# The sums of weight blocks on GpSimd, and output steps 3.5 units behind their load

## The chip, the core and the metric

The kernel runs on one core of a Trainium2 chip. The core has a matrix engine (TensorE, PE in the profile; its weight loads are PEld), a vector engine (VectorE, DVE), an activation engine (ScalarE, ACT), a general engine (GpSimd, POOL) and an engine that mostly issues transfers (SyncE, SP). Each takes its instructions in a fixed order and waits for the others through semaphores. Transfers between HBM and the on-chip memory (SBUF) are issued from the queues of SP, ACT or POOL; an instruction that stands behind a waiting one in such a queue waits with it. TensorE writes its sums to a small second memory (PSUM). The metric is the time of one execution on the device in microseconds (us).

## The reference

The kernel computes one step of a decoder layer for a prompt of 2048 tokens and 8 single-token samples, with a model width of 1024, in float32. Cut to what matters here:

```python
ada = silu(c) @ w_ada + b_ada                        # shift, scale, gate
hn = rmsnorm(x, g_norm) * (1 + scale) + shift
z = hn @ w_in                                        # xa, za | q, k, v, glr, zg
# group 1, RG-LRU: conv of 4 over xa, two gates, h_t = a_t * h_(t-1) + u_t
y_lru = h * silu(za)
# group 2, GLA: 4 heads, S_t = diag(alpha_t) S_(t-1) + k_t^T v_t, o_t = q_t S_t
y_gla = rmsnorm(o) * g_gla_norm * silu(zg)
mix = concatenate([y_lru, y_gla]) @ w_out
y = rmsnorm(x + gate * mix, g_final)
```

The final state of both groups is returned too, for the prompt and for the samples.

## The kernel before, in words

Every float32 product is made from three products of shortened numbers: each operand is split into a high part and a rest (`hh` and `hl` for the activations, two halves of a tile `w` for the weights), and high x high, high x rest and rest x high are added in PSUM. Lines 346 to 348 and 663 to 665 are these three for the values and for the other projections, line 1571 for the products of a later stage, line 1858 for the output product.

The prompt is worked on in two halves of 1024 tokens. In each half four heads of GLA (`gla_head`, in the order 3, 0, 1, 2) follow each other, and some tiles of 128 channels of the RG-LRU (`lru`) stand behind each head. A tile of the RG-LRU is projected (`project`, L663 to L665), convolved on VectorE (`conv`, L1286 and L1288), split (`xh`, `xl`, L1305 and L1306 or L1312 and L1313), sent through two gate products (`gates`, L1325 to L1328) and through a scan over the tokens (L1344). In the second half the samples' states are loaded too: per head two loads of four samples (`sample_state`, L1106 and L1108), each scaled on ScalarE (L1112) and VectorE (L1113) and used by TensorE (L1122). Between the halves the operands of some projections are put together (`gates_seven`, `lru_seven`). At the end comes the output product over the whole prompt (`Pair`, L1858).

Two places use the block form with seven products in place of eight for a 2 x 2 product of matrices. It needs sums and differences of the four blocks of a weight matrix, and these are what this document is about.

- `pair_weights` does it for six pairs of column blocks of `w_in`, in the first half. A pair is loaded to `tr` (L774, on GpSimd's queue). Then come three groups of operations: four differences (`sub`, L778), and twice two splits (`split`), each a copy `th` on ScalarE (L783), a difference on VectorE (L784) and two stores to `twd` on GpSimd's queue (L786). After the last group the next pair is loaded.
- `out_weights` does it for `w_out`, in 16 steps, six in the first half and ten in the second. `begin` (steps 0, 6 and 8) loads the gate `g` and a bias (L811, L812), which `add` sums (L817). `load` brings four blocks of 128 x 256 to `r` (L831). Then `step` multiplies them by the gate (two operations over 128 x 512, L852) in one group, and forms four differences (128 x 256, L852) in a second. Steps 4 to 7 and 12 to 15 have a third group with two splits (`p`; L856 on ScalarE, L857 on VectorE, stores on L859). `store` writes the results to `wd` (L866, on GpSimd's queue), and `again` loads the next step's blocks. The stores of the last step have to land before the output phase can load its first weights (`load_w`, L1722), as these take the same place in SBUF. The split of these weights (L1708 on ScalarE) is in the list ahead of some of the last splits of the RG-LRU.

When an operation enters the program is set by an order written out by hand. `after(units, fn)` puts `fn` into a list with a due time; `tick(units)` moves the clock on, by 1 after most projections and by 0.5 after a tile of values, and runs all entries that are due by then, in the order of due time and, at the same due time, of entry:

```python
def tick(units=1.0):
    clock[0] += units
    while pend and pend[0][0] <= clock[0]:
        heapq.heappop(pend)[2]()
```

A unit is about 24 matmuls, some 6 to 8 us. Two helpers tie a group to the place at which it enters. `behind(V)` keeps the VectorE operations inside it behind the last VectorE operation that is in the program so far, in VectorE's own order. `held(V)` makes each instruction inside it that GpSimd or SyncE executes or issues wait by a semaphore for that last VectorE operation.

In the first half the output steps end with the stop that `lru_last_a` sets. The step in work is carried to its end there, and `close_sp` starts the remaining ones in the second half. At the end of the second half the list is emptied until the last step has been stored.

Of the kernel before, what the change touches and what calls it, by code (L numbers as in the profile page):

```python
# [8 lines left out]
F32 = mybir.dt.float32  # L9
# [3 lines left out]
OP = mybir.AluOpType  # L13
# [36 lines left out]
def dram(ap, off, pattern):  # L50
    return bass.AP(tensor=ap.tensor, offset=ap.offset + off, ap=pattern)
# [3 lines left out]
def hybrid_kernel(ctx, tc, i, o):  # L55
    nc = tc.nc
    V, S, G, PE, SP = nc.vector, nc.scalar, nc.gpsimd, nc.tensor, nc.sync
# [625 lines left out]
    def behind(q):  # L683

        return tc.issue_after(next(x for x in reversed(list(nc.cur_bb.bb.instructions)) if x.engine == q.engine))


    @contextmanager
    def held(q):

        traced = nc.cur_bb.bb.instructions
        mark = next(x for x in reversed(list(traced)) if x.engine == q.engine)
        before = {id(x) for x in traced}
        yield
        for x in list(traced):
            if id(x) not in before and x.engine in (SP.engine, G.engine):
                tc.add_manual_dep(x, mark.name, mybir.DependencyInfo(
                    mybir.DependencyClass.Sync, mybir.DependencyReason.DATA), reason="held")
# [4 lines left out]
    def after(units, fn, gla=False):  # L703
        clock[1] += 1
        heapq.heappush(pend, (clock[0] + units, clock[1], fn, gla))
# [46 lines left out]
    def ready(what):  # L752
        nonlocal hp
        waiting.remove(what)
        if what == "pairs":
            hpx.close()
            hp = hpx.enter_context(tc.tile_pool(name="hp", bufs=1, reuse_waits="tile"))
        if not waiting:
            out_weights()

    def zpairs():

        return ([(ZG + 2 * h * P, ZG + (2 * h + 1) * P) for h in HEADS[1:]]
                + [(ZA + j * P, XA + j * P) for j in EARLY])

    def pair_weights(n=0):

        cols = zpairs()
        if n == len(cols):
            ready("pairs")  # L770
            return
        r = hp.tile([P, 2, KT, P], F32, tag="tr", name="tr")
        for a, col in enumerate(cols[n]):
            G.dma_start(r[:, a], i["w_in"][0, :, col:col + P].rearrange("(k p) n -> p k n", p=P))  # L774
        b11, b21, b12, b22 = r[:, 0, :4], r[:, 0, 4:], r[:, 1, :4], r[:, 1, 4:]

        def sub(x, y, z):
            return lambda: V.tensor_tensor(x, y, z, op=OP.subtract)  # L778

        def split(k, x):  # L780
            def f():
                t = hp.tile([P, 4, P], F32R, tag="th", name="th", bufs=2)
                S.copy(t, x)  # L783
                V.tensor_tensor(x, x, t.bitcast(F32), op=OP.subtract)  # L784
                for u, y in enumerate((t.bitcast(F32), x)):
                    G.dma_start(twd[n, k, :, u], y.rearrange("p k n -> p (k n)"))  # L786
            return f

        def one(ops):
            for f in ops[0]:  # L790
                with behind(V):
                    f()
            if ops[1:]:
                after(0.5, lambda: one(ops[1:]))
            else:
                pair_weights(n + 1)

        halves = [split(k, x) for k, x in enumerate((b11, b22, b12, b21))]
        after(4, lambda: one([[sub(b11, b12, b11), sub(b12, b22, b12), sub(b22, b22, b11), sub(b21, b21, b22)],
                                halves[:2], halves[2:]]))  # L800

    def out_weights(s0=0):


        def begin(s):
            q = s // 8
            outw["busy"] = True

            g = hp.tile([P, 2, 256], F32, tag="g", name="g")
            bt = hp.tile([P, 2, 256], F32, tag="t", name="bt")  # L810
            G.dma_start(g, dram(gated, (8 + 32 * q) * 256, [[0, P], [64 * 256, 2], [1, 256]]))  # L811
            G.dma_start(bt, dram(i["b_ada"], 2 * D + q * 256, [[0, P], [512, 2], [1, 256]]))  # L812
            r = load(s)

            def add():
                with behind(V):
                    V.tensor_tensor(g, g, bt, op=OP.add)  # L817
                after(0.5, lambda: step(s, r, g))

            after(4, add)  # L820

        def where(s):

            return s // 8, s // 4 % 2, s % 4

        def load(s):
            q, f, m = where(s)
            r = hp.tile([P, 2, 2, 256], F32, tag="r", name="r")
            for a in range(2):
                k = CTS[f] + 4 * a + m  # L830
                G.dma_start(r[:, a], i["w_out"][0, k * P:(k + 1) * P].rearrange("p (b n) -> p b n", b=2)[:, :, q * 256:q * 256 + 256])  # L831
            return r

        def one(ops, end):


            with behind(V):
                for f in ops[0]:
                    f()
            if ops[1:]:  # L840
                after(0.5, lambda: one(ops[1:], end))
            else:
                end()

        def step(s, r, g):
            t = hp.tile([P, 3, 256], F32, tag="t", name="t")
            b11, b12, b21, b22 = r[:, 0, 0], r[:, 0, 1], r[:, 1, 0], r[:, 1, 1]
            q, f, m = where(s)
            c = slice(q * 256, q * 256 + 256)

            def op(*a):
                return lambda: V.tensor_tensor(*a[:3], op=a[3])  # L852

            def split(n, x):
                p = hp.tile([P, 2, 256], F32R, tag="p", name="p", bufs=2)
                S.copy(p[:, 0], x)  # L856
                V.tensor_tensor(p[:, 1], x, p[:, 0].bitcast(F32), op=OP.subtract)  # L857
                for h in range(2):
                    G.dma_start(wd2[n, :, h, m, c], p[:, h].bitcast(F32))  # L859

            def store():

                for x, ops in ((r[:, 0], (B11, T1)), (r[:, 1], (B21, B22)), (t, (T2, T3, T4))):
                    for n, k in enumerate(ops):
                        if not (f and k in (B22, T4)):
                            G.dma_start(wd[f, k, :, m, c], x[:, n])  # L866
                if outw["stop"] or s == 15:
                    outw["busy"], outw["next"] = False, s + 1
                elif s % 8 < 7:
                    again(s + 1, g)  # L870
                elif q == 0:
                    begin(s + 1)

            one([[op(r[:, 0], r[:, 0], g, OP.mult), op(r[:, 1], r[:, 1], g, OP.mult)],
                 [op(t[:, 1], b22, b12, OP.subtract), op(b12, b12, b11, OP.subtract),
                  op(t[:, 0], b22, b12, OP.subtract), op(t[:, 2], b21, t[:, 0], OP.subtract)]]
                + ([[lambda: split(0, b22), lambda: split(1, t[:, 2])]] if f else []), store)

        def again(s, g):
            r = load(s)  # L880
            after(4, lambda: step(s, r, g))

        begin(s0)

# [855 lines left out]
    class Pair:  # L1740
# [157 lines left out]
        def end(self, t):  # L1898
            V.scalar_tensor_tensor(self.z[t], self.z[t], self.r[:, t:t + 1], gfin, op0=OP.mult, op1=OP.mult)
# [70 lines left out]
    for x in pairs[:2]:  # L1970
        x.new(A11)
        r = wp.tile([P, 1088], F32, tag="wr", name="wr")[:, :D].rearrange("p (q k t) -> p q k t", q=2, k=4)
# [215 lines left out]
    for n in range(2, 16):  # L2188
        g = n - 1
        x, prev = pairs[n], pairs[n - 1]  # L2190
# [16 lines left out]
    for q in range(8):  # L2207
        g, k = 2 + q // 2, q % 2
# [63 lines left out]
```

## Time and profile before

| what | value |
| --- | --- |
| median of the runs shown | 1492.54 us (1488.46 to 1494.33, 3 runs) |
| profiled execution, its own time | 1491.94 us |
| its span in the profile | 1490.2 us |
| mean granted clock of TensorE | 0.985 |
| TensorE busy | 1436.1 us, 96% |
| VectorE busy | 1058.3 us, 71% |
| ScalarE busy | 692.2 us, 46% |
| GpSimd busy, its transfer issues counted | 225.3 us, 15% |

The profile is of one execution. Its page gives the busy time of each engine and a line of 40 slices, each slice 37 us long, with the busy share in tenths; `PEclk` is the clock that TensorE was granted, in tenths of full speed. Other views group instructions by their line, list what an engine waited for, or give the instructions in order of time. `L852` is line 852 of the kernel. `r<-r,g` reads: the tile `r` is written from `r` and `g`. The busy time of VectorE, ScalarE and GpSimd counts where TensorE, which is busy nearly always, waits for them.

### The profile page before, as it was taken

The page shows a single profiled execution, that of the slowest core. Times are in us where ns is not written, and L with a number is a line of the kernel's source. Part 1 is how long each engine was busy: PE and PEld are TensorE (multiplying, and loading weights), DVE is VectorE, ACT ScalarE, POOL GpSimd, SP SyncE. Part 2 cuts the span into 40 slices and gives each one's busy share as a digit, 9 for nine tenths or more (in the row PEclk, how much of TensorE's full clock was granted, in tenths as well). Part 3 has the DMA queues.
Part 4 walks back from the last instruction along what each step waited for, and adds up shares of the span by engine and source line. Part 5 has one row for each costly group of instructions (what it writes and reads, how often), then busy time and mean ns, then how long its engine had stood idle before and what let it go on. Part 6 is the DMA issues. An engine that isn't in the chain of part 4 may idle for free.

```text
span 1490.2 us, 23612 instructions
## 1 busy us (share of the span) xinstructions
PE 1436.1 (96%) x8729; PEld 1256.3 (84%) x8729; DVE 1058.3 (71%) x2488; ACT 692.2 (46%) x1255; POOL 225.3 (15%) x374
## 2 busy tenths in 40 slices
PE   8999999999999999999999999999978999999998
PEld 6888989888898988788899998998977787778886
DVE  5757667666666779844559777686867797588886
ACT  4654544653445467533455454444437432244342
POOL 1200112211121112000212332332310000000000
PEclk9999999999999999999999999999998999999999
DMA  9655867765666454757855665565561757793452
GB/s 330 251 180 187 284 222 234 233 233 169 196 203 215 147 179 171 247 201 237 293 162 195 178 233 177 189 204 188 198 200 63 278 205 273 266 350 116 147 174 113
DMA packets 164040, 310.05 MB, mean 208 GB/s; under 512 B 13202, under 2 KB 91698, under 8 KB 161485
## 3 DMA queue, kind: packets, MB, share of 16 engines
q1 hardware_dynamic: 108197, 218.96, 42.9%
q0 software_dynamic: 23680, 73.59, 15.0%
q10 hardware_dynamic: 32048, 16.00, 3.6%
q8 instruction: 69, 1.13, 0.3%
q14 instruction: 46, 0.38, 0.1%
HBM read 191.13 MB, written 117.42 MB: 207 GB/s over the span
## 4 chain that ended last, share of the span: by engine, by line
PE 58%; DVE 15%; issue 11%; DMA 7%; ACT 7%; POOL 2%; POOLq 0%; SPq 0%; DVEq 0%; ACTq 0%
PE acc L1858 10%; PE tp L1858 7%; PE acc L663 7%; PE acc L665 7%; PE acc L664 7%; PE acc L1571 7%; PE acc L346 2%; PE acc L347 2%; PE acc L348 2%; DMA w<-wd 1%; DMA xt<-in_state_gla_dram 1%; PE po L1084 1%; DVE cv L1288 1%; DVE tg L1344 1%; ACT L989 1%
## 5 line engine op out<-in xcount | busy, mean ns | idle before, releaser
L663 PE MATMUL acc<-hh,w 128*128 128x512 f32 (+3 forms) x1080 | 375.9, 348 | 1.3 <-DVE mid L1015 1.1
L664 PE MATMUL acc<-hl,w 128*128 128x512 f32 (+3 forms) x1080 | 365.0, 338 | 0.2 <-DVE hl L205 0.2
L665 PE MATMUL acc<-hh,w 128*128 128x512 f32 (+3 forms) x1080 | 364.5, 337 | 0.0
L663 PEld LDWEIGHTS acc<-hh,w 128*128 128x128 f32 x1080 | 204.8, 190 | 19.2 <-DVE mid L1015 1.4
L664 PEld LDWEIGHTS acc<-hl,w 128*128 128x128 f32 x1080 | 205.2, 190 | 16.8 <-DVE hl L205 0.5
L665 PEld LDWEIGHTS acc<-hh,w 128*128 128x128 f32 x1080 | 204.7, 190 | 16.4 <-issue 0.4
L1858 PE MATMUL acc<-w,a 128*128 128x512 f32 (+1 forms) x792 | 186.8, 389 | 3.4 <-ACT a L1708 3.3
L1858 PEld LDWEIGHTS acc<-w,a 128*128 128x128 f32 x792 | 147.7, 189 | 37.8 <-ACT a L1708 3.7
L346 PE MATMUL acc<-w,hh 128*128 128x256 f32 (+1 forms) x508 | 145.4, 286 | 1.8 <-DMA w<-parts 1.8
L347 PE MATMUL acc<-w,hh 128*128 128x256 f32 (+1 forms) x508 | 144.1, 284 | 0.0
L348 PE MATMUL acc<-w,hl 128*128 128x256 f32 (+1 forms) x508 | 143.4, 283 | 0.0
L1858 PE MATMUL tp<-w,a 128*128 128x512 f32 x564 | 136.3, 391 | 0.4 <-DVE w L1711 0.4
L1858 PEld LDWEIGHTS tp<-w,a 128*128 128x128 f32 x564 | 105.2, 188 | 27.5 <-issue 5.2
L346 PEld LDWEIGHTS acc<-w,hh 128*128 128x128 f32 x508 | 96.6, 190 | 3.8 <-DMA w<-parts 2.0
L348 PEld LDWEIGHTS acc<-w,hl 128*128 128x128 f32 x508 | 96.8, 191 | 0.1
L347 PEld LDWEIGHTS acc<-w,hh 128*128 128x128 f32 x508 | 96.4, 190 | 0.2
L1136 ACT ACTIVATE zs<-acc 128x512 f32<-128x512 f32 (+3 forms) x70 | 34.3, 490 | 100.5 <-PE acc L665 96.8
L1288 DVE SCALAR_TENSOR_TENSOR cv<-xa,vecT,cv 128x512 f32<-128x512 f32 (+2 forms) x120 | 76.3, 642 | 6.3 <-ACT cv L1286 6.0
L1708 ACT CAST a<-s 128x512 fp32r<-128x512 f32 x61 | 36.5, 619 | 94.6 <-issue 31.6
L1137 DVE SCALAR_TENSOR_TENSOR zs<-zs,acc 128x512 f32<-128x512 f32 (+3 forms) x70 | 38.4, 549 | 44.4 <-ACT zs L1136 44.4
L965 ACT CAST vh<-acc 128x256 fp32r<-128x256 f32 x56 | 20.6, 371 | 95.0 <-PE acc L348 81.1
L966 DVE TENSOR_TENSOR vl<-acc,vh 128x256 fp32r<-128x256 f32 x56 | 23.4, 421 | 53.7 <-ACT vh L965 53.6
(404 smaller groups left out, 2813.5 us busy)
## 6 DMA issues: line engine op xcount, KB each, us to landing
parts<-w SPq DMA_DIRECT2D x37, 1024.0 KB
w<-parts SPq DMA_DIRECT2D x26, 1024.0 KB
wr<-in_w_in_dram SPq DMA_DIRECT2D x38, 512.0 KB
a<-mixd SPq DMA_DIRECT2D x63, 256.0 KB
w<-twd SPq DMA_DIRECT2D x24, 512.0 KB
w<-wd SPq DMA_DIRECT2D x12, 1024.0 KB
w<-parts SPq DMA_DIRECT2D x18, 512.0 KB
mixd<-zs ACTq DMA_DIRECT2D x35, 256.0 KB
```

The costliest lines, as they stand in the source:

```text
L346: PE.matmul(ps, hh[:, kt, c], hi[:, kt % 4], start=kt == 0, stop=False)
L347: PE.matmul(ps, hh[:, kt, c], lo[:, kt % 4], start=False, stop=False)
L348: PE.matmul(ps, hl[:, kt, c], hi[:, kt % 4], start=False, stop=kt == KT - 1)
L663: PE.matmul(ps[:, :n], hi[:, kt], a, start=kt == 0, stop=False)
L664: PE.matmul(ps[:, :n], hi[:, kt], b, start=False, stop=False)
L665: PE.matmul(ps[:, :n], lo[:, kt], a, start=False, stop=kt == KT - 1)
L1136: S.activation(z, ps, AF.Tanh, scale=0.5)
L1137: V.scalar_tensor_tensor(z, z, 1.0, ps, op0=OP.add, op1=OP.mult)
L1288: V.scalar_tensor_tensor(cv[:, cq], xa[:, cq.start + k:cq.stop + k], cw[k], cv[:, cq], op0=OP.mult, op1=OP.add)
L1571: PE.matmul(ps, w[:, u, k], x[v][k], start=start and (k, u, v) == (0, 0, 0), stop=(k, u) == (3, 1), skip_group_check=True)
L1708: S.copy(t[:, 0, k], (low(t) if src is None else src)[:, k])
L1858: PE.matmul(ps, t[:, u, k], w[:, v, k, c], start=(q < 3 or ps is own) and (k, u, v) == (0, 0, 0), stop=(k, u) == (3, 1), skip_group_check= ...
```

## The change

All operations of the two block-sum helpers that ran on VectorE or ScalarE run on GpSimd. The copies that ScalarE made by `copy` are made by a `tensor_scalar` that multiplies by one and adds zero. The groups are tied by `held(V)` in place of `behind(V)`, so that GpSimd waits at each group for the last VectorE operation before it. In `pair_weights` the whole group now stands under one `held(V)`, stores included, and the groups are 1 unit apart in place of 0.5. In `out_weights` a step is due 3.5 units behind its load in place of 4; the groups of a step are still 0.5 apart, and the wait of 4 units in `begin` stays.

```diff
         def sub(x, y, z):
-            return lambda: V.tensor_tensor(x, y, z, op=OP.subtract)
+            return lambda: G.tensor_tensor(x, y, z, op=OP.subtract)
 
         def split(k, x):
             def f():
                 t = hp.tile([P, 4, P], F32R, tag="th", name="th", bufs=2)
-                S.copy(t, x)
-                V.tensor_tensor(x, x, t.bitcast(F32), op=OP.subtract)
+                G.tensor_scalar(t, x, 1.0, 0.0, op0=OP.mult, op1=OP.add)
+                G.tensor_tensor(x, x, t.bitcast(F32), op=OP.subtract)
                 for u, y in enumerate((t.bitcast(F32), x)):
                     G.dma_start(twd[n, k, :, u], y.rearrange("p k n -> p (k n)"))
             return f
 
         def one(ops):
-            for f in ops[0]:
-                with behind(V):
+            with held(V):
+                for f in ops[0]:
                     f()
             if ops[1:]:
-                after(0.5, lambda: one(ops[1:]))
+                after(1, lambda: one(ops[1:]))
             else:
                 pair_weights(n + 1)
...
             def add():
-                with behind(V):
-                    V.tensor_tensor(g, g, bt, op=OP.add)
+                with held(V):
+                    G.tensor_tensor(g, g, bt, op=OP.add)
                 after(0.5, lambda: step(s, r, g))
...
-            with behind(V):
+            with held(V):
                 for f in ops[0]:
                     f()
...
             def op(*a):
-                return lambda: V.tensor_tensor(*a[:3], op=a[3])
+                return lambda: G.tensor_tensor(*a[:3], op=a[3])
 
             def split(n, x):
                 p = hp.tile([P, 2, 256], F32R, tag="p", name="p", bufs=2)
-                S.copy(p[:, 0], x)
-                V.tensor_tensor(p[:, 1], x, p[:, 0].bitcast(F32), op=OP.subtract)
+                G.tensor_scalar(p[:, 0], x, 1.0, 0.0, op0=OP.mult, op1=OP.add)
+                G.tensor_tensor(p[:, 1], x, p[:, 0].bitcast(F32), op=OP.subtract)
                 for h in range(2):
                     G.dma_start(wd2[n, :, h, m, c], p[:, h].bitcast(F32))
...
         def again(s, g):
             r = load(s)
-            after(4, lambda: step(s, r, g))
+            after(3.5, lambda: step(s, r, g))
```

## The prediction

> **What bounds the kernel now.** I read the page first (engines, then the slices), then the waits of TensorE, then the granted clock by stretches, and last the rows around each long wait.
>
> ```profile
> PE 1436.1 (96%) x8729; PEld 1256.3 (84%) x8729; DVE 1058.3 (71%) x2488; ACT 692.2 (46%) x1255; POOL 225.3 (15%) x374
> PE   8999999999999999999999999999978999999998
> PEclk9999999999999999999999999999998999999999
> ```
>
> TensorE is busy for 96% of the span, with two thinner slices near three quarters of it (1118 to 1192 us). VectorE at 71% and GpSimd at 15% bound nothing as a whole. Whatever the change does to VectorE, ScalarE and GpSimd reaches the end only through an idle stretch of TensorE. Inside the blocks' stages (143 to 1110 us) and just behind them, the long ones are these, in TensorE's timeline (start, length, work, in brackets the idle time before it and what ended it):
>
> ```profile
> 276.70 1.22 PE L1325 MATMUL acc<-xh,wg 128*128 128x512 f32 x2 [3.18 <-ACT xh L1312]
> 924.86 1.08 PE L1122 MATMUL po<-xt,qm 128*32 128x256 f32 x8 [3.08 <-DVE xt L1113]
> 1029.00 0.94 PE L1050 MATMUL tp<-xb,e 128*128 128x128 f32 x6 [2.69 <-DVE xb L1035]
> 1090.05 0.64 PE L1122 MATMUL po<-xt,qm 128*32 128x256 f32 x8 [2.91 <-DVE xt L1113]
> 1120.79 1.01 PE L1325 MATMUL acc<-xh,wg 128*128 128x384 f32 x2 [8.16 <-ACT xh L1305]
> ```
>
> Each costs more than its idle time. By stretches (us, then busy time of PE, PEld, DVE, ACT, POOL, the granted clock, DMA share, GB/s):
>
> ```profile
> 276.80:282.40 5.60, 5.60 (x13) 4.38 (x14) 4.90 (x14) 4.60 (x7) 0.89 (x1) 0.50 0.68 190
> 1030.00:1033.40 3.40, 3.40 (x13) 3.40 (x12) 1.72 (x6) 3.35 (x8) 0.73 (x1) 0.50 0.92 304
> 1091.40:1094.80 3.40, 3.40 (x13) 3.39 (x12) 2.31 (x12) 3.37 (x5) 0.00 (x0) 0.50 0.48 165
> 1120.80:1128.90 8.10, 7.47 (x22) 5.83 (x23) 6.17 (x11) 7.15 (x15) 0.00 (x0) 0.50 0.21 87
> ```
>
> The reader is to see the 0.50 behind each idle stretch: at half clock half of the stretch is lost, 2.8 us at 277, 1.7 at 1030, 1.7 at 1091, 4.0 at 1121. A wait of 2.7 us thus costs about 4.4. The Trainium skill (TensorE: Matmul & The Clock Gate, Part 1) says that activity is judged in free-running windows of about 3.4 us; the two 3.4 us rows agree, and by it an idle stretch of this size loses the clock only if it lies unluckily.
>
> **The change part by part.** Taken off: busy time of seven lines over the whole run (same columns, but of that line alone, so the time stands under DVE or ACT): L778, L784, L817, L852, L857 on VectorE, then L783, L856 on ScalarE.
>
> ```profile
> 0.00:1490.20 1490.20, 16.49 (x24) 0.99 0.62 208
> 0.00:1490.20 1490.20, 15.68 (x24) 0.99 0.62 208
> 0.00:1490.20 1490.20, 2.05 (x3) 0.99 0.62 208
> 0.00:1490.20 1490.20, 47.48 (x96) 0.99 0.62 208
> 0.00:1490.20 1490.20, 6.46 (x16) 0.99 0.62 208
> 0.00:1490.20 1490.20, 14.74 (x24) 0.99 0.62 208
> 0.00:1490.20 1490.20, 6.47 (x16) 0.99 0.62 208
> ```
>
> So 88.2 us leave VectorE and 21.2 leave ScalarE, of the 1490. By shape (from the code) that is, in two-input operations, 48 + 3 + 32 = 83 of 512 columns and 64 + 16 = 80 of 256; in copies 24 of 512 and 16 of 256.
>
> Put on GpSimd: a one-input operation of 512 columns has rows, and so has what happens when VectorE works at the same time. GpSimd, then VectorE, both in the timeline:
>
> ```profile
> 582.08 1.12 POOL L204 TENSOR_SCALAR hh<-fs 128x512 fp32r<-128x512 f32 x1 [1.23 <-ACT fs L201]
> 600.05 0.62 POOL L204 TENSOR_SCALAR hh<-fs 128x512 fp32r<-128x512 f32 x1 [1.34 <-DVE fs L203]
> ```
>
> ```profile
> 581.31 0.74 DVE L1288 SCALAR_TENSOR_TENSOR cv<-xa,vecT,cv 128x512 f32<-128x512 f32 x1
> 582.05 0.68 DVE L205 TENSOR_TENSOR hl<-fs,hh 128x512 fp32r<-128x512 f32 x1
> 582.65 1.09 DVE L1288 SCALAR_TENSOR_TENSOR cv<-xa,vecT,cv 128x512 f32<-128x512 f32 x1
> ```
>
> Alone the operation takes 0.62 us. Started beside a two-input VectorE operation it takes 1.12, about until that one ends (582.05 + 0.68) plus its own 0.62, and the next VectorE operation then takes 1.09 in place of 0.74. The two engines take turns. No row shows a two-input operation on GpSimd: it lies between 0.62 (as one input) and 1.24 us (two inputs read in turn), 0.31 to 0.62 for 256 columns; I take the upper ends, since the row has one operand to fetch and the new form two. That is 83 x 1.24 + 80 x 0.62 + 24 x 0.62 + 16 x 0.31 = 102.9 + 49.6 + 14.9 + 5.0 = 172 us on GpSimd, and by the lower ends 96. The Trainium skill (GPSIMD Engine Reference, elementwise side by side) has 4497 ns for 2048 columns of a two-input add; as an estimate 1.12 us for 512, and 157 us in all. What that does to VectorE is read from the stages:
>
> ```profile
> 143.00:340.00 197.00, 190.02 (x1270) 170.81 (x1269) 136.52 (x296) 103.84 (x178) 37.85 (x63) 0.98 0.70 232
> 366.00:556.00 190.00, 190.00 (x1053) 165.88 (x1052) 132.25 (x284) 92.21 (x151) 35.92 (x63) 1.00 0.58 189
> 990.00:1110.00 120.00, 113.88 (x833) 109.04 (x833) 89.86 (x309) 53.65 (x121) 35.90 (x62) 0.97 0.59 193
> ```
>
> In the first, VectorE works 136.5 of 197 us, 32 of them on the blocks; what stays is 104, or 0.53. If GpSimd's 172 us meet a VectorE that wants the port for half of the time, VectorE loses some 90 us and has been given 88: a wash in load. The bounds are a gain of 88 (they never meet) and a loss of 84 (they always do). In the first stage GpSimd's share is 48 x 1.24 + 24 x 0.62 = 74 us; at worst VectorE is at (104 + 74) / 197 = 0.90 and GpSimd at (38 + 74) / 197 = 0.57, so neither becomes the bound. The cover is TensorE's other products: in the second stage it is busy for 190.0 of 190 us beside all this. What is left is single places.
>
> The pace: the order list counts units and looks at its entries at each tick, mostly a whole unit. A wait of 1 in place of 0.5 between the groups of a pair therefore ends at the same tick, but the entry then stands behind gates due at that tick, not ahead. 3.5 in place of 4 changes nothing where a step's last group ended on a whole unit and no half tick follows; by the ticks it moves steps 2 to 5 and 11 to 15 ahead by half a unit or one, up to some 8 us. Their r loads and stores on GpSimd's queue move with them. The first six steps still fall before the stop, so that work is not redistributed. All this costs nothing while no TensorE operand comes from it; where it does:
>
> (a) 276 us. VectorE loses one block operation (0.7) and ScalarE two copies (1.2) from the chain to `xh`: -1.8. But the groups now sit behind the gates' last operations, beside the convolution that ends the wait: a copy, a two-input operation and another copy, 0.62 + 1.24 + 0.62 = 2.5. Net +0.7; bounds -4.6 (the wait falls to 1.4 and the 2.8 of half clock go) and +2.5.
>
> (b) 924 and 1090 us. Both wait for the second state load, which stands in GpSimd's queue behind a step's stores and next loads:
>
> ```profile
> 915.54 1.44 POOL L831 DMA_DIRECT2D r<-in_w_out_dram  x2 [2.50 <-DMA wd<-r]
> 916.97 0.78 POOL L1108 DMA_DIRECT2D xt<-in_state_gla_dram  x1
> 1078.01 1.44 POOL L831 DMA_DIRECT2D r<-in_w_out_dram  x2
> 1080.62 0.76 POOL L1108 DMA_DIRECT2D xt<-in_state_gla_dram  x1
> ```
>
> At 916 the step keeps its tick (step 9). Its four subtractions take 4 x 0.62 = 2.5 us on GpSimd, ahead of the stores, where stores now slip in between; the state load and TensorE come later by 1.5 (0 to 3.5). At 1078 step 14 is one tick earlier, so its loads have passed: -2 (0 to -4.6, the wait under 1.5 and the 1.7 of half clock gone).
>
> (c) 1029 us. Two products with the gate stand in VectorE right ahead of `xb`:
>
> ```profile
> 1027.19 1.28 DVE L852 TENSOR_TENSOR r<-r,g 128x512 f32<-128x512 f32 x2
> 1028.39 0.55 DVE L1035 SCALAR_TENSOR_TENSOR xb<-acc,xb 128x384 f32<-128x384 f32 x1
> ```
>
> Without them the wait is 1.5, and the 1.7 of half clock may go: -2.9. But they now run a tick earlier on GpSimd, 2 x 1.24, possibly ahead of the state load of that place, whose arrival starts the same chain: then +1.3. I take -1.
>
> (d) The last step, 1121 us. The chain of waits, with GpSimd's last issue and SyncE's wait:
>
> ```profile
> 1108.48 1.07 POOL L859 DMA_DIRECT2D wd<-p  x2 [0.88 <-ACT p L856]
> SPq L1722 <- DMA wd<-p: 5.0, 1, 5.0
> 1113.38 5.19 DMA w<-wd
> 1118.67 1.14 ACT w L1708 x2
> ```
>
> ```profile
> 1097.49 0.69 DVE L852 TENSOR_TENSOR r<-r,g 128x512 f32<-128x512 f32 x1
> 1098.10 1.23 DVE L1341 SCALAR_TENSOR_TENSOR tg<-xl,tg 128x1032 f32<-128x1032 f32 x1
> 1101.33 2.35 DVE L1344 TENSOR_TENSOR_SCAN tg<-xl,hc,tx 128x1024 f32<-128x1024 f32 x1
> ```
>
> The first weights of the last phase are loaded (5.2 us) when the last step's stores have landed, as they take its place; ScalarE splits them ahead of `xh`, and TensorE has stood for 8.16 us. Now the two products start a tick earlier. The other eight operations (4 x 0.62 + 2 x 0.31 + 2 x 0.62 = 4.3 us) alternate with VectorE's long ones, and seven stores of 0.54 follow or slip between: 8.1 us from 1097.5 (where VectorE has the step's work now) if nothing blocks, and 13.5 if each operation waits out one of VectorE's (8 x 0.7, an estimate between 0.69 and 2.35), so the last issue ends between 1105.6 and 1111.0 (now 1109.6). I take the later end, as VectorE has no pause there: +1.4 on the wait and +1 of half clock, +2.4 (-4 to +5).
>
> (e) New short waits where GpSimd holds the port for 1.24 us and VectorE held itself for 0.68: +1 (0 to +8).
>
> Sum: 0.7 + 1.5 - 2 - 1 + 2.4 + 1 = +2.6 on the profiled run's 1491.9 (span 1490.2 and 1.7 around it): 1494.5. The median of the runs shown is 1492.5, 0.6 above that run.
>
> **The rivals.** Faster: the port turns are hidden and the three middle waits fall under 2 us, without their half clock: -4.6, -2.9, -4.6 make -12, with (d) as forecast about -10, so 1482. For it: all three lie within 3.2 us. Against: GpSimd's work returns to the same spots.
>
> Slower through the last step: only (d). From where the stores land 4 us later, the wait is 12.2 and one or two more stretches of 3.4 us run at half clock: +4 +1.7 to 3.4, near 1500. Then it decides alone; 1497 to 1502. For it: VectorE's unbroken row there. Against: the earlier products.
>
> Slower through the port: an engine twice as slow holds it longer, and in the convolution chains of 143 to 340 and 870 to 1110 us three new waits of 2.7 us appear, each with 1.7 of half clock: 3 x 4.4 = +13, so 1505. The Trainium skill (SBUF — State Buffer, Who interferes with whom) calls the pair of ports that the two share an exclusive lock for the whole instruction; the 1.12 and 1.09 above agree. Against: from 366 to 556 us TensorE has no idle time at all, so most waits there have slack.
>
> **How the numbers follow.** A measurement of this kernel tells about 0.5%, 7.5 us, from no change. Forecast (within 0.5%) 0.47; faster 0.20; last step 0.15; port 0.15; slower in a way not listed 0.03. The likeliest one's own range is 1487 to 1500. For 8 in 10 the range reaches into both sides: 1481 to 1508. Faster 0.20, same 0.47, slower 0.33.
>
> **What would show it.** VectorE's busy time down by less than 88 us, with single two-input operations near 1.2 to 1.9 us; GpSimd's up by 150 to 220 with waits inside; two-input 512-column operations there at 1.1 to 1.3 us where alone; the idle stretch before `xh` near 1121 us 8 to 11 us long; those at 1029 and 1090 shorter. I am wrong if two-input operations on GpSimd take far from 1.2 us, if a new wait of over 2.7 us stands between 366 and 556 us, or if TensorE's matmuls themselves grow.

## The result, and the profile after

The changed kernel takes 1507.6 us (median of 4 runs, 1504.4 to 1509.4) against 1490.5 (4 runs) for the kernel before: a ratio of 1.011, 95% interval 1.008 to 1.014. It is slower by 16 to 17 us. The span of the profiled execution grew from 1490.2 to 1506.5 us.

The page of the kernel after, engines and slices:

```profile
PE 1440.1 (96%) x8729; PEld 1255.7 (83%) x8729; DVE 1061.3 (70%) x2325; ACT 673.2 (45%) x1215; POOL 439.4 (29%) x577
PE   8999998799999999999999999989996999999998
PEclk9999999899999999999999999999998999999999
```

VectorE's instructions fell from 2488 to 2325, but its busy time did not fall: 1061.3 us against 1058.3. Without the 88.2 us that the moved operations had cost there (five of the seven lines, the other two ran on ScalarE) it would be about 970, so some 91 us were added to other instructions. GpSimd grew by 214 us. TensorE has a new thin place at slices 7 and 8 (226 to 301 us), and a lesser one at slice 27 (979 to 1017).

TensorE's timeline of the kernel after, with the rows that answer to those of before and most of the longest new ones (start, length, instruction, in brackets the idle time and what ended it):

```profile
240.91 0.39 PE L1080 MATMUL po<-vh,amh 128*128 128x256 f32 x1 [2.93 <-DVE on L1089]
258.88 1.33 PE L1170 MATMUL tp<-ident,on 128*128 128x128 f32 x6 [1.68 <-DVE on L1097]
286.73 0.80 PE L1325 MATMUL acc<-xh,wg 128*128 128x512 f32 x1 [7.86 <-ACT xh L1312]
935.70 0.64 PE L1122 MATMUL po<-xt,qm 128*32 128x256 f32 x8
1002.85 0.88 PE L1170 MATMUL tp<-ident,on 128*128 128x128 f32 x3 [2.52 <-DVE on L1097]
1043.93 1.32 PE L1050 MATMUL tp<-xb,e 128*128 128x128 f32 x6 [1.62 <-DVE xb L1035]
1054.97 0.61 PE L1172 MATMUL tp<-sel,os 128*128 128x8 f32 x4 [2.23 <-DVE os L1132]
1105.30 0.64 PE L1122 MATMUL po<-xt,qm 128*32 128x256 f32 x8 [0.20 <-PE acc L665]
1112.06 0.50 PE L1172 MATMUL tp<-sel,os 128*128 128x8 f32 x3 [1.87 <-DVE os L1132]
1139.37 1.01 PE L1325 MATMUL acc<-xh,wg 128*128 128x384 f32 x2 [9.13 <-ACT xh L1305]
```

Where the time came in is read by setting the start of the same product in both kernels against each other: at `acc` L1325 it is 276.70 and 286.73, so 10.0 us are lost by then. At L1050 (1029.00 and 1043.93) it is 14.9, at L1122 (1090.05 and 1105.30) 15.2, at the last L1325 (1120.79 and 1139.37) 18.6, and at the end 16.3. Some 60% is lost among the pair blocks of the first half, 5 us among the output steps of the second, 3 just ahead of the last phase, of which 2 come back. The waits for the second state load are gone (the L1122 rows, which had 3.08 and 2.91), and the one at L1050 is shorter (2.69 before).

How the 7.86 us came about is seen in VectorE's timeline, before and after. Kernel before:

```profile
270.18 2.29 DVE L1344 TENSOR_TENSOR_SCAN tg<-xl,tx 128x1024 f32<-128x1024 f32 x1
272.38 0.14 DVE L1351 TENSOR_TENSOR tg<-xl,vecT 128x8 f32<-128x8 f32 x1
...
275.25 0.75 DVE L1288 SCALAR_TENSOR_TENSOR cv<-xa,vecT,cv 128x512 f32<-128x512 f32 x1
275.91 0.17 DVE L681 COPY mixs<-zs 128x8 f32<-128x8 f32 x1
275.99 0.48 DVE L1288 SCALAR_TENSOR_TENSOR cv<-xa,vecT,cv 128x256 f32<-128x256 f32 x1
```

Kernel after, VectorE:

```profile
276.43 3.26 DVE L1344 TENSOR_TENSOR_SCAN tg<-xl,tx 128x1024 f32<-128x1024 f32 x1
279.62 1.16 DVE L1351 TENSOR_TENSOR tg<-xl,vecT 128x8 f32<-128x8 f32 x1
...
284.27 1.75 DVE L1288 SCALAR_TENSOR_TENSOR cv<-xa,vecT,cv 128x512 f32<-128x512 f32 x1
285.94 1.96 DVE L681 COPY mixs<-zs 128x8 f32<-128x8 f32 x1
287.82 1.34 DVE L1288 SCALAR_TENSOR_TENSOR cv<-xa,vecT,cv 128x256 f32<-128x256 f32 x2
```

and GpSimd in the same stretch, with three operations (at 214, 562 and 955 us) from places where VectorE stood still:

```profile
214.08 1.29 POOL L784 TENSOR_TENSOR tr<-tr,th 128x512 f32<-128x512 f32 x1
...
275.38 5.37 POOL L778 TENSOR_TENSOR tr<-tr 128x512 f32<-128x512 f32 x2
...
286.58 1.29 POOL L784 TENSOR_TENSOR tr<-tr,th 128x512 f32<-128x512 f32 x1
...
561.93 0.40 POOL L856 TENSOR_SCALAR p<-r 128x256 fp32r<-128x256 f32 x1 [0.33 <-DVE xl L1313]
...
955.37 0.74 POOL L852 TENSOR_TENSOR t<-r 128x256 f32<-128x256 f32 x1
```

From the scan to the last 256-column `cv` the kernel before takes 5.8 us (270.18 to 275.99), the kernel after 11.4 (276.43 to 287.82), with the same instructions and no block operation on VectorE in either. They stand still behind each other. The two L778 take 5.37 us in place of 2 x 1.29, the second until a microsecond after the scan has ended (276.43 + 3.26). The scan itself takes 3.26 us in place of 2.29, a `cv` of 512 columns 1.75 in place of 0.75. A copy of 8 columns (L681) takes 1.96 us and ends at 287.90, as the L784 of 286.58 does at 287.87. `xh`, which TensorE waits for, is made from this `cv`.

### The profile page after: what moved, and what is told of

Its sections match the earlier page's. It is cut to its first block, busy times and chain, and to the rows that moved or that the text cites. A ratio compares the mean times of both kernels' runs of the same rounds, so it can differ in the third digit from the quotient of the medians.

```text
span 1506.5 us, 23486 instructions
## 1 busy us (share of the span) xinstructions
PE 1440.1 (96%) x8729; PEld 1255.7 (83%) x8729; DVE 1061.3 (70%) x2325; ACT 673.2 (45%) x1215; POOL 439.4 (29%) x577
## 4 chain that ended last, share of the span: by engine, by line
PE 63%; DVE 16%; DMA 7%; ACT 6%; issue 4%; POOL 3%; SPq 1%; DVEq 0%; POOLq 0%; ACTq 0%
PE acc L1858 10%; PE tp L1858 7%; PE acc L663 7%; PE acc L665 7%; PE acc L664 7%; PE acc L1571 6%; PE acc L346 3%; PE acc L347 3%; PE acc L348 3%; DVE cv L1288 1%; DMA w<-wd 1%; PE po L1084 1%; PE tp L1170 1%; DVE xb L1007 1%; ACT L989 1%
## 5 line engine op out<-in xcount | busy, mean ns | idle before, releaser
L663 PEld LDWEIGHTS acc<-hh,w 128*128 128x128 f32 x1080 | 205.2, 190 | 17.6 <-ACT tx L1328 1.1
L1288 DVE SCALAR_TENSOR_TENSOR cv<-xa,vecT,cv 128x512 f32<-128x512 f32 (+2 forms) x120 | 85.6, 717 | 7.6 <-ACT cv L1286 6.9
L852 POOL TENSOR_TENSOR r<-r,g 128x512 f32<-128x512 f32 x32 | 44.6, 1414 | 92.9 <-DVE zs L1137 45.9
```

The source lines that it names most:

```text
L663: PE.matmul(ps[:, :n], hi[:, kt], a, start=kt == 0, stop=False)
L852: return lambda: G.tensor_tensor(*a[:3], op=a[3])
L1288: V.scalar_tensor_tensor(cv[:, cq], xa[:, cq.start + k:cq.stop + k], cw[k], cv[:, cq], op0=OP.mult, op1=OP.add)
```

## The experiments

Two questions: which part of the change costs the time, and whether it is the turns at a shared port, GpSimd's own queue, the place of the groups in the order list or the pace.

**Each helper alone.** The first kernel takes only `pair_weights` from the change, the second only `out_weights`, with its 3.5:

Pairs alone, against the changed kernel (in `out_weights` all of the change is taken back):

```diff
-                    G.tensor_tensor(g, g, bt, op=OP.add)
+                    V.tensor_tensor(g, g, bt, op=OP.add)
...
-                return lambda: G.tensor_tensor(*a[:3], op=a[3])
+                return lambda: V.tensor_tensor(*a[:3], op=a[3])
...
-            after(3.5, lambda: step(s, r, g))
+            after(4, lambda: step(s, r, g))
```

Output steps alone (in `pair_weights` all of the change is taken back):

```diff
-            return lambda: G.tensor_tensor(x, y, z, op=OP.subtract)
+            return lambda: V.tensor_tensor(x, y, z, op=OP.subtract)
...
-                after(1, lambda: one(ops[1:]))
+                after(0.5, lambda: one(ops[1:]))
```

> Only the pair blocks (pair_weights) are changed: their arithmetic on GpSimd, their groups a whole unit apart; the output steps stay on VectorE and ScalarE at 4 units. Theory A (the two engines take turns at a shared port, and in the pair blocks' stage this lands in the convolution chain): about +10 of the changed kernel's +16 us are here, 1499 to 1503 us, with the wait of about 7.9 us at acc L1325 near 285 us and new waits of over 1.5 us near 240 and 258 us. Theory B (the output steps carry it, by GpSimd's work in their stores' queue or by the pace): 1489 to 1494 us. The changed kernel's last-phase wait at L1325 is then back at about 8.2 us in both.

> Only the output steps (out_weights) are changed: arithmetic on GpSimd and 3.5 units; the pair blocks stay on VectorE and ScalarE, half a unit apart. Theory A: the rest of the +16, so +5 to +7, 1495 to 1498 us, spread over several waits of 0.5 to 2.5 us between 840 and 1065 us and a last-phase wait near 9 us. Theory B: nearly all of it, 1503 to 1508 us.

Measured: pairs alone 1513.8 us (ratio to before 1.016, 1.014 to 1.019), output steps alone 1501.6 (1.009, 1.006 to 1.012). The first lies above both of its ranges; the second lies between its two, 4 us above that of theory A. TensorE's timeline of the pairs alone, and VectorE's:

```profile
288.12 1.22 PE L1325 MATMUL acc<-xh,wg 128*128 128x512 f32 x2 [7.86 <-ACT xh L1312]
386.90 1.39 PE L1170 MATMUL tp<-ident,on 128*128 128x128 f32 x5 [11.37 <-DVE on L1097]
```

```profile
380.61 0.69 DVE L817 TENSOR_TENSOR g<-g,bt 128x512 f32<-128x512 f32 x1 [11.95 <-DMA r<-in_w_out_dram]
```

The first wait is that of the full change. The second accounts for about 11 us and so for the miss: the first sum of the output steps, still on VectorE here, stands 12 us for loads that GpSimd issues only when its pair work is done, with all of VectorE behind it. The full change does not have this, as its sum waits on GpSimd. Moving one helper alone thus makes a cost of its own, and the two parts cannot be added. In the output steps alone the wait near 277 is as before; the loss comes from new waits like that at 1048, and the wait before the last phase is 9.37 us, as in the full change:

```profile
277.30 1.22 PE L1325 MATMUL acc<-xh,wg 128*128 128x512 f32 x2 [3.18 <-ACT xh L1312]
1047.88 0.90 PE L1172 MATMUL tp<-sel,os 128*128 128x8 f32 x4 [3.50 <-DVE os L1132]
1132.54 1.01 PE L1325 MATMUL acc<-xh,wg 128*128 128x384 f32 x2 [9.37 <-ACT xh L1305]
```

So both helpers cost time, each in its own stage. One unforeseen wait aside, the expectation that the pairs carry most of it is not confirmed by these two; the runs with memsets below divide it better.

**The pace taken back.**

```diff
-            after(3.5, lambda: step(s, r, g))
+            after(4, lambda: step(s, r, g))
```

> The changed kernel with 4 units between an output step and its load in place of 3.5; all arithmetic stays on GpSimd. Theory A: the engine and not the pace costs the time, so within 4 us of the changed kernel, 1503 to 1511 us, and the wait for the second state load near 924 us and that near 1090 us may come back. Theory C (the earlier steps collide with the state loads and gates): 1495 to 1500 us.

Measured: 1530.4 us (1.028, 1.025 to 1.031). No theory said that: the half unit is worth 23 us of gain inside the changed kernel. TensorE's timeline:

```profile
941.51 1.08 PE L1122 MATMUL po<-xt,qm 128*32 128x256 f32 x8 [4.69 <-DVE xt L1113]
1117.17 0.66 PE L1122 MATMUL po<-xt,qm 128*32 128x256 f32 x4 [4.97 <-DVE xt L1113]
1156.82 0.69 PE L1325 MATMUL acc<-xh,wg 128*128 128x384 f32 x1 [16.48 <-ACT xh L1305]
```

and GpSimd ahead of the first of them:

```profile
924.51 0.85 POOL L852 TENSOR_TENSOR t<-r 128x256 f32<-128x256 f32 x1 [7.08 <-DVE on L1097]
...
933.46 0.78 POOL L1108 DMA_DIRECT2D xt<-in_state_gla_dram  x1
```

At 4 units the step's second group waits 7 us on GpSimd for its place behind VectorE, and the state load stands behind it in the same queue. GpSimd then stands 14.8 us for the place of the last step's products (until 1133.1), and that step's stores come so late that TensorE stands for 16.5 us before the last phase.

**GpSimd writes but does not read.** Each operation is replaced by two memsets of its target, in all blocks. A memset fills a tile with a constant and takes no tile as input; the sums and splits themselves are left out, so this kernel serves for its time alone. Cut to the first of the places:

```diff
+    def blank(x):
+        for v in (0.02, 0.01):
+            G.memset(x, v)
...
-            return lambda: G.tensor_tensor(x, y, z, op=OP.subtract)
+            return lambda: blank(x)
```

> The changed kernel with each arithmetic operation on GpSimd replaced by two memsets of the same target, so GpSimd reads no SBUF operand; the blocks' values are thus left out and the output is not the reference's. Places, order, stores and waits stay. Theory A (turns at a shared read port): VectorE's two-input operations are as short as before (512-column cv at 0.74 to 0.78 us, L1344 at 2.3 us), the wait at acc L1325 near 285 us falls below 4 us, and the time is 1486 to 1496 us. Theory D (the delay is GpSimd's own queue and the place of the work behind the gates, not the port): the time stays above 1500 us and the 7.9 us wait above 6 us. Two memsets of 512 columns are estimated at 0.6 to 1.2 us together, from the one-input 0.62 us; that they read nothing makes them shorter than the two-input operations, at most by half, so a fall to 1498 to 1502 would be undecided.

Measured: 1476.1 us, 0.991 of before (0.988 to 0.993) and 31.5 us under the changed kernel, 10 us below the range of theory A. The L1325 wait near 276 is 1.89 us (line numbers are 4 higher here):

```profile
275.63 0.99 PE L1329 MATMUL acc<-xh,wg 128*128 128x512 f32 x2 [1.89 <-ACT xh L1316]
```

The groups of VectorE show what GpSimd's reads cost (busy time, mean ns of one); kernel before, after, and with memsets:

```profile
L1288 DVE SCALAR_TENSOR_TENSOR cv<-xa,vecT,cv 128x512 f32<-128x512 f32 x57 | 42.8, 752 | 3.2 <-ACT cv L1286 3.0
L1086 DVE TENSOR_SCALAR S<-S,f 128x256 f32<-128x256 f32 x60 | 21.1, 351 | 0.0
```

```profile
L1288 DVE SCALAR_TENSOR_TENSOR cv<-xa,vecT,cv 128x512 f32<-128x512 f32 x57 | 47.9, 840 | 3.7 <-ACT cv L1286 3.1
L1086 DVE TENSOR_SCALAR S<-S,f 128x256 f32<-128x256 f32 x60 | 28.7, 479 | 0.0
```

```profile
L1292 DVE SCALAR_TENSOR_TENSOR cv<-xa,vecT,cv 128x512 f32<-128x512 f32 x57 | 42.5, 745 | 3.5 <-ACT cv L1290 2.8
L1090 DVE TENSOR_SCALAR S<-S,f 128x256 f32<-128x256 f32 x60 | 40.6, 677 | 0.0
```

The convolution's operation with two SBUF inputs is back at 745 ns once GpSimd does not read. Taken one by one, the trace says more. In the changed kernel 13 of the 57 lie beside GpSimd arithmetic for 0.2 us or more, and take 1161 ns in the mean; the 44 that lie clear of it take 745. With memsets six lie beside them for as long, and take 742. So neither GpSimd's queue nor the place of its work lengthened these instructions, but its reads. The Trainium skill (SBUF — State Buffer, Who interferes with whom) says the same: a VectorE instruction with two SBUF inputs collides with a GpSimd instruction that reads SBUF, not with one that only writes. By its next rule one-input operations in a two-port mode collide with either, and the trace agrees as far as it goes: L1086, with one tensor input, takes 352 ns clear of GpSimd, 906 in the mean beside its arithmetic (13 of them) and 1377 beside memsets (19). That L1086 runs in such a mode is not shown. VectorE's busy time is 1015.4 us here, 45 above the 970 that were left to it, so writes alone bring back about half as much busy time as the changed kernel's operations do.

At the wait near 276 the place of GpSimd's work changed too. VectorE's chain has its old length there, 5.8 us from the scan to the last `cv` (269.10 to 274.92), but the memsets that stand for the four subtractions now end before the scan:

```profile
269.10 2.29 DVE L1348 TENSOR_TENSOR_SCAN tg<-xl,tx 128x1024 f32<-128x1024 f32 x1
274.84 0.16 DVE L681 COPY mixs<-zs 128x8 f32<-128x8 f32 x1
```

```profile
256.30 3.78 POOL L768 MEMSET tr<- 128x512 f32 x8 [3.68 <-DVE zs L1141]
```

In the changed kernel GpSimd came to this pair later (it issued the second load of `tr` at 265.58, here at 251.72), so its subtractions lay beside the scan. Of the 5.6 us by which that chain was longer, 2.0 lie in the scan and the L1351 behind it, where GpSimd is idle in this run; some 3.5 lie beside the splits, whose memsets begin at 272.91 here, beside the same convolution, and lengthen nothing. For this larger part the reads are shown to be the cause; in the smaller one GpSimd's delay in its own queue has a share.

Not all of the 31.5 us is the port either: the memsets take 164 us on GpSimd (48.9 + 31.0 + 27.2 + 25.8 + 17.6 + 10.2 + 3.3 by groups), the operations that they stand for 188 alone, and GpSimd's busy time, with its own waiting in it, fell from 439.4 to 377.3 us, so that whatever stands behind in its queue comes earlier. How the 31.5 us divide between the two this run can't say.

**Memsets in one helper, operations in the other.** Against the changed kernel, in the first run:

```diff
-            return lambda: G.tensor_tensor(x, y, z, op=OP.subtract)
+            return lambda: blank(x)
...
-                G.tensor_scalar(t, x, 1.0, 0.0, op0=OP.mult, op1=OP.add)
-                G.tensor_tensor(x, x, t.bitcast(F32), op=OP.subtract)
+                blank(t.bitcast(F32))
+                blank(x)
```

and in the second:

```diff
-                return lambda: G.tensor_tensor(*a[:3], op=a[3])
+                return lambda: blank(a[0])
...
-                G.tensor_tensor(p[:, 1], x, p[:, 0].bitcast(F32), op=OP.subtract)
+                blank(p[:, 1].bitcast(F32))
```

> The changed kernel with the pair blocks' operations alone as two memsets of the same target (their values are left out, so the output is not the reference's); the output steps read and compute on GpSimd as in the changed kernel. With both as memsets the time fell from 1507.5 to 1476. Theory A (each stage pays its own port turns): the pairs' part comes back, so the wait of 7.9 us near 285 us falls under 3 and the time to 1490 to 1497 us, while the short waits from 800 to 1120 us and the 9.1 us before the last phase stay. Theory F (the loss is passed on: what the first stage saves is lost again behind it): 1500 to 1507 us.

> The changed kernel with the output steps' operations alone as two memsets of the same target (values left out); the pair blocks read and compute on GpSimd. Theory A: the 7.9 us near 285 us stays, the short waits from 800 to 1060 us shrink to a third, and the time is 1487 to 1494 us, so that this and the run with the pairs as memsets add up to the 31 us within 6. Theory F: 1500 to 1507 us.

Measured: 1494.8 us with the pairs as memsets (ratio to before 1.004, 1.002 to 1.005), 1491.9 with the output steps (1.002, 1.001 to 1.003). Both lie in the range of theory A. That is 12.8 and 15.7 us below the changed kernel; together 28.5 of the 31.5. (With each time set against that of the kernel before that was measured beside it, the gains are 11, 14 and 30 us.) Each stage pays for itself, and little is passed on. The wait before the last phase stays at 9.06 us with the pairs as memsets and is 7.83 with the output steps. The wait of 7.86 us follows the pairs alone: TensorE with the pairs as memsets, then with the output steps:

```profile
275.08 0.73 PE L1329 MATMUL acc<-xh,wg 128*128 128x512 f32 x2 [2.33 <-ACT xh L1316]
```

```profile
287.30 1.22 PE L1329 MATMUL acc<-xh,wg 128*128 128x512 f32 x2 [7.82 <-ACT xh L1316]
```

**The place of the pair groups.**

```diff
-                after(1, lambda: one(ops[1:]))
+                after(0.5, lambda: one(ops[1:]))
```

> The changed kernel with half a unit between the groups of a pair, as before, in place of a whole one; the pair arithmetic stays on GpSimd. Theory A (port turns, wherever the groups lie in the convolution chain): 1500 to 1510 us, with a wait of over 5 us still at acc L1325 near 285 us. Theory D (the groups' new place behind the gates, beside the convolution that ends the wait): the 7.9 us wait falls to about 3 to 4 us, and with its half clock 6 to 8 us are gone: 1498 to 1502 us.

Measured: 1512.0 us (1.016, 1.014 to 1.017), 2 us above the range of theory A. The wait is still there, with others at new places:

```profile
199.49 0.38 PE L1082 MATMUL po<-vh,aml 128*128 128x256 f32 x1 [2.66 <-DVE aml L1057]
288.78 0.80 PE L1325 MATMUL acc<-xh,wg 128*128 128x512 f32 x1 [7.16 <-ACT xh L1312]
349.34 0.58 PE L1082 MATMUL po<-vh,aml 128*128 128x256 f32 x1 [3.12 <-DVE aml L1057]
```

So the place behind the gates was not the cause; a group on GpSimd delays the chain at either place. Here the splits lie mostly ahead of the scan, and it is the three long VectorE operations there (L1341, L305, L1342) that take 2.31, 2.53 and 1.75 us in place of 1.22 to 1.23.

**The copies back on ScalarE.**

```diff
-                G.tensor_scalar(t, x, 1.0, 0.0, op0=OP.mult, op1=OP.add)
+                S.copy(t, x)
```

> The changed kernel with the 40 copies back on ScalarE; the 163 two-input operations stay on GpSimd. The copies take 0.62 (24) and 0.40 us (16) on GpSimd alone, 21 us in all, of 217. Theory A (port turns by two-input and one-input operations alike, in proportion to GpSimd's time): up to a tenth of the contention's 31 us comes back, 1502 to 1508 us. Theory E (the copy puts ScalarE's chain to xh back in the way, and GpSimd must now wait for ScalarE between copy and subtraction, with its queue's stores and loads behind): 1508 to 1516 us.

Measured: 1558.2 us (1.048, 1.046 to 1.049), far beyond both. ScalarE's row and TensorE's:

```profile
197.45 0.62 ACT L783 CAST th<-tr 128x512 fp32r<-128x512 f32 x1 [15.74 <-POOL tr L778]
```

```profile
206.31 1.01 PE L1050 MATMUL tp<-xb,e 128*128 128x128 f32 x3 [16.13 <-DVE xb L1035]
381.34 1.01 PE L1050 MATMUL tp<-xb,e 128*128 128x128 f32 x3 [14.49 <-DVE xb L1035]
```

The copy stands at the head of ScalarE's queue for 15.7 us until GpSimd has made its operand, and the chain to `xb` stands behind it. At this place in the order the copies had to go along with the arithmetic.

**Other paces, on both versions.** 3.5 and 3 units with the arithmetic on VectorE; 3 in the changed kernel; and 3 with only the output steps on GpSimd. The edit is this line, with 3.5 or 3 in place of 4:

```diff
-            after(4, lambda: step(s, r, g))
+            after(3, lambda: step(s, r, g))
```

> The kernel before with 3.5 units in place of 4 and nothing else: all arithmetic stays on VectorE and ScalarE. In the changed kernel the half unit was worth about -23 us (1530 at 4, 1507.5 at 3.5). Theory A (the gain of the half unit is the state loads' place in GpSimd's queue, whoever does the arithmetic): the waits for the second state load near 924 and 1090 us fall under 1.5 us, so 1480 to 1486 us. Theory B (the gain exists only where arithmetic stands in that queue): within 3 us of before, 1486 to 1492 us. Theory C (the steps' products with the gate come nearer to the operands of other chains on VectorE): 1493 to 1500 us.

> The changed kernel with 3 units between a step and its load in place of 3.5. If the place of the steps in GpSimd's queue against the state loads is what 3.5 mends, 3 moves each step by another tick or none: 1500 to 1515 us, with no wait of over 2.5 us for a state load. If instead the chain is steep (each half unit is 23 us as from 4 to 3.5), 1484 to 1490 us. If the last step's products now meet its r load, which takes 3 to 10 us to land, GpSimd's queue stops there: 1515 to 1530 us.

> The kernel before with 3 units in place of 4 (all arithmetic on VectorE and ScalarE). By the order list seven steps instead of six then end before the stop, and the last one ends 12 units earlier. In the changed kernel 3 took the wait of 9.1 us before the last phase to under 1, for 4.5 us at a state load near 942. If the same happens here: 8 us of wait and some 5 us of half clock less, about 3 us more at the state load: 1476 to 1482 us. If a step's products now stand in VectorE's queue ahead of a load that has not landed: over 1488 us.

> Output steps alone on GpSimd, with 3 units; the pair blocks stay on VectorE and ScalarE. At 3.5 units this was 1501.6 us, and the changed kernel fell by 9.6 us from 3.5 to 3. Theory A: 1490 to 1494 us, so still above the kernel before with 3 units by the output steps' own port turns, 8 to 15 us. If GpSimd's arithmetic costs nothing once the steps lie early enough: 1476 to 1483 us, the same as the kernel before with 3 units.

Measured:

| units | arithmetic on VectorE and ScalarE | on GpSimd (output steps and pairs) | output steps alone on GpSimd |
| --- | --- | --- | --- |
| 4 | 1488 to 1489 | 1530.4 | |
| 3.5 | 1486.9 (0.999, 0.998 to 1.000) | 1507.6 | 1501.6 |
| 3 | 1477.8 (0.992, 0.991 to 0.994) | 1497.9 (1.007, 1.006 to 1.009) | 1488.7 (1.000, 0.999 to 1.002) |

The first column at 4 is the kernel before, as measured beside these runs. With 3 units, 1477.8 us as expected (1476 to 1482), it is the fastest complete kernel of the case, 0.8% under its time with 4 and 2% under the changed kernel. At equal pace the engines' change costs 42, 21 and 20 us. At 3 units the last step is done earlier, and TensorE no longer stands before the last phase; kernel before with 3, then the changed kernel with 3:

```profile
1109.63 0.44 PE L1325 MATMUL acc<-xh,wg 128*128 128x384 f32 x1 [0.89 <-ACT tx L1328]
```

```profile
942.25 0.70 PE L1122 MATMUL po<-xt,qm 128*32 128x256 f32 x8 [4.52 <-DVE xt L1113]
...
1129.48 0.44 PE L1325 MATMUL acc<-xh,wg 128*128 128x384 f32 x1 [0.86 <-ACT tx L1328]
```

The changed kernel with 3 came out between two of its cases: better than the first by 2 us, and with a state-load wait of 4.52 us that this case excluded. The output steps on GpSimd still cost 11 us at 3 units (1488.7 against 1477.8, 1 us below the range of theory A), and the pairs 9 more. With 3.5 units the kernel before gains 1 us (interval 0 to 3), as theory B had it, and not the 1480 to 1486 us of theory A. The wait for the state load at 1090 does go (0.17 us), but the one near 925 is still 2.29 us, and the one at L1050 grows from 2.69 to 3.92.

## Why the prediction was right and wrong

The measured time lies at the upper edge of the range, and 13 us above the number given. That it lies inside at all is luck: the range ends at 1508, two of the four runs are above that, and the likeliest case was to end at 1500. What happened is nearest to the rival "slower through the port" (1505 us), which got 0.15. It had the cause, but not its places: in place of three new waits of 2.7 us one old wait grew by 4.7, six new ones of 1.7 to 2.9 us came (240.91 to 1112.06; one of 1.95 us at 979.80 is not among the rows above), and three old ones shrank by 6.9 in all.

- **Off VectorE, on GpSimd: right in load.** 90 us lost on VectorE against 88 given was forecast, and 91 were measured. Part of this is chance: GpSimd's operations take 188 us by the sum below in place of 172, and the same half of that would have given 100. Two-input operations of 512 columns take 1.29 us alone (forecast 1.24). Those of 256 take 0.74, above the bound of 0.62: halving the columns doesn't halve the time. By the measured values the operations take 83 x 1.29 + 80 x 0.74 + 24 x 0.62 + 16 x 0.40 = 188 us; with GpSimd's own waiting at the port busy time grew by 214, inside the 150 to 220 that was named. The estimate from the Trainium skill (GPSIMD Engine Reference, elementwise side by side), 1.12 us and 157 in all, was further off.
- **"A wash in load" read as no delay: the step that failed.** The 88 us left from operations that had slack, and the 91 us came back on whatever VectorE ran beside GpSimd, the convolution and scan among it, for which TensorE waits: with its reads left out the kernel takes 1476.1 us, though a part of that gain is GpSimd's shorter work. An average over a stage (VectorE 0.53 busy) could not show this.
- **(a), 276 us: mis-sized.** +0.7 was forecast, from three GpSimd operations put behind the gates. The chain itself was stretched from 5.8 to 11.4 us, the wait grew from 3.18 to 7.86, and with new waits of 2.93 and 1.68 ahead of it the loss by then is 10.0 us. The prediction added GpSimd's 2.5 us and left VectorE's own instructions at their old lengths. The named reason (place behind the gates) is refuted by the half-unit run.
- **(b), state loads: half right.** At 1090 us -2 was forecast, and the wait fell from 2.91 to 0.20. At 924 us +1.5 was forecast, and there is no wait at all. With 4 units the changed kernel waits 4.69 us there, so inside the change the half unit took this wait away, in a step that the prediction let keep its tick.
- **(c), 1029 us: right.** -1 forecast; the wait went from 2.69 to 1.62 and its half clock stayed (granted clock 0.50 from 1044.30 to 1047.70).
- **(d), the last step: right in size.** +1.4 forecast on the wait, 1.0 measured.
- **(e), new short waits: mis-sized.** +1 was forecast. Between 287 and 1105 us the net loss is 15.2 - 10.0 = 5.2 us, though the three waits of (b) and (c) shrank by 3.1 + 2.7 + 1.1 = 6.9. The new ones, 2.52 and 2.23 the longest, thus cost at least 12, above the bound of 8.
- **The pace "costs nothing": wrong inside the change.** Alone it is worth about 1 us, as the 3.5 on the kernel before shows. With arithmetic in GpSimd's queue it is worth 23: the rows at 4 units show state loads and the last stores behind arithmetic that waits for VectorE. The prediction treated the two parts as independent.

## What to carry to other kernels

Work moved from VectorE to GpSimd need not relieve VectorE: here 88 us were taken off it, and 91 came back in other instructions, nearly all of it in those that ran beside GpSimd's. What matters is which of these lie in a chain that the bounding engine waits for, so price the stretched chain and not the stage's mean load. A queue that issues loads shouldn't carry arithmetic that waits for another engine, unless the loads stand far enough ahead. When a change has an engine part and a small timing part, try the timing part alone, and further than the change takes it: with the arithmetic left where it was, 3.5 units gave 1 us and 3 units 11.

## What the runs showed of the hardware

GpSimd holds up even the smallest VectorE instructions: a copy of 8 columns took 1.96 us in place of 0.17, and an 8-column product 1.16 in place of 0.14, while a GpSimd operation ran, and ended with it (the copy had begun 0.6 us ahead of that operation, while GpSimd issued a store). GpSimd's time is not proportional to the columns: two inputs 1.29 us for 512 and 0.74 for 256, and one input 0.62 and 0.40. Beside GpSimd operations that read, the two-input convolution took 1161 ns in the mean in place of 745; beside ones that only write it took 742, while a one-input operation (L1086) went from 352 to 1377.
